# A two-layer hybrid transformer block: x feature-major in the first stage, the modulation matrix in transfers of 2 MB, first projection group of 768 columns

## The chip, the core and the metric

One NeuronCore of a Trainium2 chip runs the whole program. Its engines are TensorE (PE: matrix products into PSUM, the accumulation memory; PEld is its loading of the stationary operand), VectorE (DVE), ScalarE (ACT), GpSimd (POOL) and SyncE (SP), whose queue issues all DMA transfers here. The metric is device time in microseconds (us); lower is better. TensorE's clock is granted at one of two levels, 1.2 or 2.4 GHz; a profile gives the granted clock as a share of the higher one.

## What is computed

```
for l in range(2):                                   # x is 1024 x 2048, f32
    mod = silu(c) @ w_mod[l] + b_mod[l]              # one row, 3 * 2048 columns
    shift, scale, gate = split(mod, 3)
    h = rms_norm(x, g_pre[l]) * (1 + scale) + shift
    proj = h @ w_in[l]                               # 2048 x 5648
    a_q, a_k, a_v, s_u, s_v, c_q, c_k, c_v, c_g, z = split(proj)
    y_a = sliding_window_attention(rope(a_q), rope(a_k), a_v, sinks)
    y_b = gelu(s_u) * mix(layer_norm(gelu(s_v)))     # per 128 tokens
    y_c = rms_norm(gated_linear_attention(c_q, c_k, c_v, log_sigmoid(c_g @ w_up + b)))
    out = (concat(y_a, y_b, y_c) * silu(z)) @ w_out[l]
    x = x + gate * rms_norm(out, g_post[l])
```

`rms_norm(x, g)` is `x / sqrt(mean(x * x) + 1e-6) * g`, the mean taken over the 2048 features of a token.

## The kernel before

The work is cut into four phases (layer 0 and 1, each in two halves of 512 tokens). A phase runs all column groups of `w_in` (mostly 512 columns) and then of `w_out`; attention, gating and linear attention of the phase run beside them as generators that are stepped on by a count of products (`tick`). A projection is done at near f32 accuracy: each operand is split into a high and a low part (ScalarE casts the high part, VectorE subtracts it to get the low one), and for each 128x128 tile of weights and each K tile (128 of the 2048 features, 16 in all) TensorE runs three products, high by high, high by low and low by high (`mm_f`, lines 382 to 384). Instructions are written in program order; a scheduler then sets the order on each engine, and each engine runs its list strictly in that order.

The change touches the first stage alone, which prepares layer 0, tokens 0 to 511. There 8 chunks of `w_mod` (each 16 K tiles by 512 columns, 4 MB: the shift and scale of 256 features) come in 64 transfers of 2 K tiles (tiles `wm`, line 1107's operands; `WM0` = 9 buffers). Each K tile of a chunk is multiplied by `scb` (silu(c), 32 equal columns) into one of four strips of 32 partitions of a PSUM tile; `mod_acc` takes a copy (L1117), four products with the identity matrix turn it (L197), and short VectorE operations make `acol` and `bcol`, the scale and shift per feature (`mod_columns`). x stands token-major in `xg`: ScalarE squares it with a sum per token (L1054), `finish_stats` makes `rstd`, GpSimd multiplies it in (L283), TensorE turns each tile with the identity matrix (L1084), and VectorE and ScalarE make the split operand `act` (L1086, L278, L279). Two K tiles become ready with each chunk.

Between these, generator `work` runs the first projection group, 640 columns in 5 PSUM tiles (`psk`; the products' stationary tiles come from `whl` and, for the fifth, `hl_b`), one step per piece of a chunk. The remaining 128 of the 768 key, query and linear-attention key columns are a group of their own straight after, and then comes the group `vcg` of 272 columns, token-major (lines 390 to 392). `rope_tables(0)` (position angles, sine and cosine: 18 VectorE operations, two sines on ScalarE, two stores on SyncE) is issued at the start of the stage. PSUM has 6 tiles `pj` and 2 tiles `mx`.

Of the kernel before, what the change touches and what calls it, by code (L numbers as in the profile page):

```python
# [10 lines left out]
F32 = mybir.dt.float32  # L11
# [25 lines left out]
WM0 = 9  # L37
# [3 lines left out]
def hybrid_kernel(ctx: ExitStack, tc: tile.TileContext, a, y_out):  # L41
# [82 lines left out]
    def rsqrt(out, src, n):  # L124

        i = sm.tile([P, n], I32, tag="rq_i", name="rq_i")
# [3 lines left out]
        for it in range(3):  # L130
            w = sm.tile([P, n], F32, tag="rq_w", name="rq_w")
            V.tensor_tensor(w, yv, yv, ALU.mult)
            V.scalar_tensor_tensor(w, w, -0.5, src, ALU.mult, ALU.mult)
            dst = out if it == 2 else sm.tile([P, n], F32, tag="rq_y", name="rq_y")
            V.scalar_tensor_tensor(dst, w, 1.5, yv, ALU.add, ALU.mult)
            yv = dst
# [156 lines left out]
    def h_filler_x(h, slots):  # L293
# [456 lines left out]
    def in_phase(l, h, slots, pre=None):  # L750
# [29 lines left out]
        ps = ps[4:] + proj_f(P, slots) if pre else proj_f(256, slots)  # L780
        ck = evac(2, hold, ps)
# [225 lines left out]
    with tc.tile_pool(name="start", bufs=1) as st:  # L1007
        scb = st.tile([P, NK, 32], F32, name="scb")
        V.tensor_copy(scb, sc.unsqueeze(2).broadcast_to([P, NK, 32]))
        xg = [st.tile([P, 4, NT, P], F32, name=f"x0_{g}") for g in range(4)]  # L1010
        ss0 = sm.tile([P, NT, 4], F32, tag="xss4", name="xss4")
        load(mb[0], a["b_mod_col"][0])
        load(gpc[0], a["g_pre"][0])
        ws = deque()
        raw_a, raw_b, hl_a, hl_b = deque(), deque(), deque(), deque()

        def first_load(c):
            if c < 8:
                k = slice(c * KC, (c + 1) * KC)
                pool, tag = (st, "raw_a") if c % 3 == 2 else (wraw_p, "wraw")  # L1020
                r = pool.tile([P, KC, 512], F32, tag=tag, name="raw_a")
                load(r, a["w_in"][0, 0, :, k])
                raw_a.append(r)
                r = st.tile([P, KC, P], F32, name="raw_b", bufs=3)
                load(r, a["w_ck"][0, :, k, 0:P])
                raw_b.append(r)

        def first_split(c):
            if c < 8:
                for raw, hls, cols in ((raw_a, hl_a, 512), (raw_b, hl_b, P)):  # L1030
                    r = raw.popleft()
                    if cols == P:
                        hl = st.tile([P, 2, KC, P], F32R, name="hl_b", bufs=2)
                    else:
                        hl = whl_p.tile([P, 2, KC, 512], F32R, tag="whl", name="whl")
                    S.copy(hl[:, 0], r)
                    V.tensor_tensor(hl[:, 1], r, hl[:, 0].bitcast(F32), ALU.subtract)
                    hls.append(hl)
# [6 lines left out]
        for i in range(WM0 - 1):  # L1045
            mod_load(i)
        for g in range(4):
            load(xg[g], a["x"][0, 4 * g:4 * g + 4].rearrange("j p t c -> p j t c"))
        for _ in rope_tables(0):
            pass  # L1050
        first_load(0)
        for g in range(4):
            for t in range(NT):
                S.activation(junk_tile().rearrange("p (j c) -> p j c", j=4), xg[g][:, :, t], AF.Square,  # L1054
# [217 lines left out]
```

## Time and profile before

| | |
|---|---|
| runs | median 3127.75 us of 3 (3121.66 to 3129.04) |
| profiled execution, its own time | 3122.08 us |
| its span, first to last instruction | 3120.4 us |
| TensorE busy | 3042.7 us of the span |
| mean granted clock | 0.991 |

Rows of the profile are read like this: `L382` is line 382 of the kernel, a line can be a helper's; `out<-in` are the names of tiles; `x8` is a count. A time in square brackets is what the engine idled just before, and what ended that. On TensorE each f32 product of `scb` appears as two records, so a transfer of 2 K tiles is 4 records. Records of products overlap: the start of the next one, not the length, gives the pace.

### The profile page before, as it was taken

To read this page: it belongs to the slowest core of one execution; us is meant where nothing else is said; L and a number is where in the kernel's file an instruction comes from. 1 tells how busy PE (TensorE), PEld (TensorE's weight loads), DVE (VectorE), ACT (ScalarE), POOL (GpSimd) and SP (SyncE) were. 2 spreads that over 40 slices of the span, in tenths; PEclk is the share of its full clock that TensorE was granted. 3 is DMA by queue.
4 is the path that set the end of the run, shared out by engine and by line. 5 is a ranking of instruction groups with operands and counts; after the bars stand their busy time and mean duration, and the time that the engine had idled before them with its cause. 6 is when DMAs were issued, how large, how long until landed. Compare 5 with 4: busy or idle time off the path is not lost.

```text
span 3120.4 us, 44382 instructions
## 1 busy us (share of the span) xinstructions
PE 3042.7 (98%) x17346; PEld 2448.0 (78%) x17346; DVE 1837.3 (59%) x2957; ACT 1206.2 (39%) x2399; POOL 43.4 (1%) x84
## 2 busy tenths in 40 slices
PE   6999999999999999999999999999999999999998
PEld 2477778888878787888888878788888888788886
DVE  3358768565676877745355676644346486663425
ACT  3145437332344443423234554432223544442323
POOL 2000000000000000000000000000000000000000
PEclk8999999999999999999999999999999999999999
DMA  9754446566676435544446323334446332343535
GB/s 330 240 163 140 145 135 206 169 203 203 200 237 197 131 120 178 173 135 149 122 123 190 95 75 94 115 109 142 119 124 203 97 89 85 108 120 113 164 107 165
DMA packets 224195, 468.99 MB, mean 150 GB/s; under 512 B 21584, under 2 KB 77296, under 8 KB 223984
## 3 DMA queue, kind: packets, MB, share of 16 engines
q1 hardware_dynamic: 223984, 466.15, 48.7%
q8 instruction: 136, 2.23, 0.3%
q14 instruction: 75, 0.61, 0.1%
HBM read 429.37 MB, written 36.70 MB: 149 GB/s over the span
## 4 chain that ended last, share of the span: by engine, by line
PE 82%; DVE 8%; DMA 5%; ACT 2%; issue 2%; SPq 0%; DVEq 0%; ACTq 0%
PE pj L382 13%; PE pj L383 12%; PE pj L384 12%; PE pj L390 12%; PE pj L392 12%; PE pj L391 12%; DMA wm<-in_w_mod_dram 2%; PE mx L546 2%; PE mx L492 2%; PE pj L1107 1%; DVE whl L369 1%; DMA t<-in_gla_norm_g_dram 1%; DVE ma L225 1%; DMA t<-in_x_dram 1%; PE mx L533 1%
## 5 line engine op out<-in xcount | busy, mean ns | idle before, releaser
L369 DVE TENSOR_TENSOR whl<-wraw,whl 128x1024 fp32r<-128x1024 f32 (+3 forms) x512 | 590.6, 1154 | 730.6 <-ACT whl L368 728.0
L368 ACT CAST whl<-wraw 128x1024 fp32r<-128x1024 f32 (+3 forms) x512 | 509.1, 995 | 1097.0 <-PE pj L392 515.5
L390 PE MATMUL pj<-whl,act 128*128 128x512 f32 (+1 forms) x2048 | 785.5, 384 | 1.0 <-ACT whl L368 1.0
L392 PE MATMUL pj<-whl,act 128*128 128x512 f32 (+1 forms) x2048 | 777.8, 380 | 0.0
L391 PE MATMUL pj<-whl,act 128*128 128x512 f32 (+1 forms) x2048 | 775.3, 379 | 1.2 <-DVE whl L369 1.2
L382 PE MATMUL pj<-act,whl 128*128 128x512 f32 x1904 | 751.6, 397 | 3.6 <-ACT whl L368 2.0
L383 PE MATMUL pj<-act,whl 128*128 128x512 f32 x1904 | 745.3, 391 | 0.3 <-DVE act L279 0.3
L384 PE MATMUL pj<-act,whl 128*128 128x512 f32 x1904 | 744.5, 391 | 0.5 <-DVE whl L369 0.5
L392 PEld LDWEIGHTS pj<-whl,act 128*128 128x128 f32 x2048 | 385.4, 188 | 73.2 <-issue 1.2
L390 PEld LDWEIGHTS pj<-whl,act 128*128 128x128 f32 x2048 | 385.3, 188 | 72.7 <-issue 5.6
L391 PEld LDWEIGHTS pj<-whl,act 128*128 128x128 f32 x2048 | 385.5, 188 | 68.5 <-DVE whl L369 1.9
L382 PEld LDWEIGHTS pj<-act,whl 128*128 128x128 f32 x1904 | 357.5, 188 | 101.3 <-issue 20.3
L384 PEld LDWEIGHTS pj<-act,whl 128*128 128x128 f32 x1904 | 358.1, 188 | 83.7 <-issue 7.1
L383 PEld LDWEIGHTS pj<-act,whl 128*128 128x128 f32 x1904 | 358.2, 188 | 77.7 <-issue 6.2
L225 DVE SCALAR_TENSOR_TENSOR ma<-wm,sc,ma 128x512 f32<-128x512 f32 x240 | 179.7, 749 | 102.5 <-DMA wm<-in_w_mod_dram 100.1
L517 ACT ACTIVATE M<-M,at_nm 128x128 f32<-128x128 f32 x256 | 99.4, 390 | 46.7 <-DVE at_nm L509 42.2
L535 DVE TENSOR_TENSOR PT<-mx,amask 128x1024 f32<-128x1024 f32 x64 | 78.1, 1220 | 22.6 <-PE mx L533 22.6
L1107 PE MATMUL pj<-wm,scb 128*32 128x512 f32 x256 | 67.0, 665 | 24.2 <-DMA wm<-in_w_mod_dram 24.2
L501 DVE COPY_PREDICATED M<-pmask,mx 128x256 f32<-128x256 uint8 x128 | 51.6, 442 | 57.3 <-ACT M L500 48.5
L546 PE MATMUL mx<-PT,v 128*64 128x128 f32 x960 | 68.4, 288 | 13.9 <-DVE PT L535 13.9
L546 PEld LDWEIGHTS mx<-PT,v 128*64 128x64 f32 x960 | 57.5, 143 | 28.3 <-DVE PT L535 16.3
L500 ACT COPY M<-mx 128x256 f32<-128x256 f32 x96 | 32.1, 375 | 101.0 <-PE mx L492 100.7
(230 smaller groups left out, 2421.9 us busy)
## 6 DMA issues: line engine op xcount, KB each, us to landing
wraw<-in_w_in_dram SPq DMA_DIRECT2D x312, 512.0 KB, 3.6
wraw<-in_w_out_dram SPq DMA_DIRECT2D x136, 512.0 KB, 3.6
wm<-in_w_mod_dram SPq DMA_DIRECT2D x256, 256.0 KB, 3.3
wm<-in_w_mod_dram SPq DMA_DIRECT2D x64, 512.0 KB, 6.2
y<-at SPq DMA_DIRECT2D x64, 256.0 KB, 2.7
q<-y SPq DMA_DIRECT2D x64, 256.0 KB, 3.3
q<-x SPq DMA_DIRECT2D x36, 256.0 KB, 2.8
wraw<-in_w_vcg_dram SPq DMA_DIRECT2D x32, 272.0 KB, 2.8
```

The source lines that it names most:

```text
L225: V.scalar_tensor_tensor(acc, ws[k], sc[:, k:k + 1], acc, ALU.mult, ALU.add)
L368: S.copy(hl[:, 0], raw)
L369: V.tensor_tensor(hl[:, 1], raw, hl[:, 0].bitcast(F32), ALU.subtract)
L382: PE.matmul(ps, lhsT=whi, rhs=slot[:, 0], start=(k == 0), stop=False)
L383: PE.matmul(ps, lhsT=whi, rhs=slot[:, 1], start=False, stop=False)
L384: PE.matmul(ps, lhsT=wlo, rhs=slot[:, 0], start=False, stop=(k == NK - 1))
L390: PE.matmul(ps, lhsT=slot[:, 0, c], rhs=whi, start=(k == 0), stop=False)
L391: PE.matmul(ps, lhsT=slot[:, 0, c], rhs=wlo, start=False, stop=False)
L392: PE.matmul(ps, lhsT=slot[:, 1, c], rhs=whi, start=False, stop=(k == NK - 1))
L517: S.activation(Mf[:, k], Mf[:, k], AF.Exp, bias=nm[:, k:k + 1], scale=0.125, accum_out=den[:, k:k + 1])
L546: PE.matmul(yp[64 * p:64 * p + 64, n * P:(n + 1) * P], lhsT=vv[:, g * 64:g * 64 + 64], rhs=pts[p][:, w, n], start=(w == 0), stop=(w == 1 o ...
L1107: PE.matmul(mps[r:r + 32, :], lhsT=scb[:, k], rhs=w[:, kk], start=(k < 4), stop=(k >= 12))
```

## The change

- x of the first half is loaded feature-major (`xq`, from `x_f`, which now holds both halves) ahead of `w_mod`. Its squares are summed over the features by 8 products with a matrix of ones (`sums`), and 1/sqrt is taken on a tile of 128x512 (`r0`; `rsqrt` now works in place and in a given pool). The split operand is made from `xq` directly: times `acol` times `r0`, plus `bcol` (three operations for a K tile). The squares with sums per token, `rstd` of this half, GpSimd's products and the 64 turns of x are gone.
- A chunk of `w_mod` comes as two transfers of 8 K tiles (2 MB) in 3 buffers, and its products run 8 K tiles in a row.
- Weights of the first group come K tile by K tile (512 columns of `w_in` and 256 of `w_ck`), each queued behind a half chunk; the group has 768 columns in 6 PSUM tiles, and the separate group of 128 columns is gone. The PSUM tile of the modulation moves from `pj` to `mx`.
- The order is written out: half chunk, projection of a K tile, half chunk, columns and operands, projection of a K tile. `rope_tables(0)` moves from the start of the stage to behind chunk 5.

```
         def fetch():
-                load(xt, a["x_f"][len(xs)])
+                load(xt, a["x_f"][1, len(xs)])
...
-        ps = ps[4:] + proj_f(P, slots) if pre else proj_f(256, slots)
-        ck = evac(2, hold, ps)
+        ck = evac(2, hold, ps[4:] if pre else proj_f(256, slots))
...
         if (l, h) == (0, 0):
-            seq = [(a["w_ck"][l, :, :, P:], P)] + seq[2:]
+            seq = seq[2:]
...
+        xq = [act_p.tile([P, 2, H], F32, tag="act", name="xq") for _ in range(8)]
+        for c in range(8):
+            load(xq[c], a["x_f"][0, 2 * c:2 * c + 2].rearrange("j p t -> p j t"))
...
+        def first_load(k):
+            if k < NK:
+                r = wraw_p.tile([P, 1, 768], F32, tag="wraw", name="wraw")
+                load(r[:, 0, 0:512], a["w_in"][0, 0, :, k])
+                load(r[:, 0, 512:], a["w_ck"][0, :, k])
+                raw_q.append(r)
...
-        def mod_load(i):
-            if i < 64:
-                w = st.tile([P, 2, 512], F32, name="wm0", bufs=WM0)
-                load(w, a["w_mod"][0, i // 8, :, 2 * (i % 8):2 * (i % 8) + 2])
+        def mod_load(c, part):
+            if c < 8:
+                w = st.tile([P, 8, 512], F32, name="wm0", bufs=3)
+                load(w, a["w_mod"][0, c, :, 8 * part:8 * part + 8])
                 ws.append(w)
...
+        sums = mxt()
+        for c in range(8):
+            sq = st.tile([P, 2, H], F32, name="sq", bufs=2)
+            S.activation(sq, xq[c], AF.Square)
+            s2 = st.tile([P, H], F32, name="s2", bufs=2)
+            V.tensor_tensor(s2, sq[:, 0], sq[:, 1], ALU.add)
+            PE.matmul(sums, lhsT=ones, rhs=s2, start=(c == 0), stop=(c == 7))
+        r0 = st.tile([P, H], F32, name="r0")
+        V.tensor_scalar(r0, sums, 1.0 / D, EPS, ALU.mult, ALU.add)
+        rsqrt(r0, r0, H, st)
+        psk = [pjt() for _ in range(6)]
...
+        def fill(c, mps):
+            acc = st.tile([P, 512], F32, name="mod_acc", bufs=2)
+            S.copy(acc, mps)
             mod_columns(0, c, acc, 4)
+            for j in range(2):
+                k = 2 * c + j
+                xt, b = t2(), bcol[0][:, k:k + 1]
+                V.scalar_tensor_tensor(xt, xq[c][:, j], acol[0][:, k:k + 1], r0, ALU.mult, ALU.mult)
+                s = act_p.tile([P, 2, 512], F32R, tag="act", name="act")
+                S.activation(s[:, 0], xt, AF.Identity, bias=b)
+                V.scalar_tensor_tensor(s[:, 1], xt, b, s[:, 0].bitcast(F32), ALU.add, ALU.subtract)
+                slots.append(s)
...
         for c in range(8):
+            if c:
+                mod_load(c, 1)
+                first_load(2 * c - 1)
+            mps = mxt()
+            mod_products(mps, 0)
+            if c:
+                project(2 * c - 2)
+                mod_load(c + 1, 0)
+                first_load(2 * c)
+            mod_products(mps, 1)
+            with urgent():
+                fill(c, mps)
+            if c:
+                project(2 * c - 1)
+            if c == 5:
+                for _ in rope_tables(0):
+                    pass
```

TensorE, around the end of a chunk's products (`wm0` by `scb`, into the modulation's PSUM tile) and the turn of `mod_acc`, before (numbers behind names are those of buffers):

```order
L1107 MATMUL pj_286<-wm0_723,scb_167 32x512 x2
L383 MATMUL pj_284<-act_824,whl_692 128x512
L384 MATMUL pj_284<-act_824,whl_692 128x512
L382 MATMUL pj_285<-act_824,hl_b_695 128x512
L1107 MATMUL pj_286<-wm0_730,scb_167 32x512 x2
L383 MATMUL pj_285<-act_824,hl_b_695 128x512
L384 MATMUL pj_285<-act_824,hl_b_695 128x512
L1107 MATMUL pj_286<-wm0_737,scb_167 32x512 x2
L1107 MATMUL pj_286<-wm0_744,scb_167 32x512 x2
L197 MATMUL mx_877<-ident_81,mod_acc_858 128x128 x4
L1084 MATMUL mx_896<-ident_81,x0_2_171 128x128 x4
L1107 MATMUL pj_286<-wm0_759,scb_167 32x512 x2
```

And with the change, around the second half of a later chunk (`L1067` are the products with `scb`, 8 K tiles in one row; `L381` to `L383` the three products of a projection):

```order
L1067 MATMUL mx_489<-wm0_484,scb_185 32x512 x8
L381 MATMUL pj_254<-act_460,whl_555 128x512
L382 MATMUL pj_254<-act_460,whl_555 128x512
L381 MATMUL pj_255<-act_460,whl_555 128x512
L196 MATMUL mx_534<-ident_81,mod_acc_532 128x128 x4
L383 MATMUL pj_254<-act_460,whl_555 128x512
L382 MATMUL pj_255<-act_460,whl_555 128x512
L383 MATMUL pj_255<-act_460,whl_555 128x512
L381 MATMUL pj_256<-act_460,whl_555 128x512
L382 MATMUL pj_256<-act_460,whl_555 128x512
L383 MATMUL pj_256<-act_460,whl_555 128x512
```

The products with `scb` stood in runs of 2 K tiles between single projections; they now stand in a run of 8, and the turns of x (`L1084`) are gone.

SyncE's queue over one chunk of the stage, before:

```order
L58 DMA raw_a_591<-in_w_in_dram 128x1024
L58 DMA raw_b_593<-in_w_ck_dram 128x2x128
L58 DMA wm0_598<-in_w_mod_dram 128x1024
L58 DMA wm0_616<-in_w_mod_dram 128x1024
L58 DMA wm0_623<-in_w_mod_dram 128x1024
L58 DMA wm0_630<-in_w_mod_dram 128x1024
L58 DMA wm0_637<-in_w_mod_dram 128x1024
L58 DMA wm0_652<-in_w_mod_dram 128x1024
L58 DMA wm0_659<-in_w_mod_dram 128x1024
L58 DMA wm0_677<-in_w_mod_dram 128x1024
L58 DMA raw_a_698<-in_w_in_dram 128x1024
L58 DMA raw_b_700<-in_w_ck_dram 128x2x128
```

And with the change, from K tile 10's weights on (`wm0` are the half chunks, `t2_760` is the load of the positions, `cs0_0` and `cs0_1` the stores of the two tables):

```order
L57 DMA wraw_705<-in_w_in_dram 128x512
L57 DMA wraw_705<-in_w_ck_dram 128x256
L57 DMA t2_760<-in_positions_dram 128x512
L57 DMA wm0_788<-in_w_mod_dram 128x4096
L57 DMA wraw_790<-in_w_in_dram 128x512
L57 DMA wraw_790<-in_w_ck_dram 128x256
L57 DMA wm0_823<-in_w_mod_dram 128x4096
L57 DMA cs0_0_99<-t2_768 128x512
L57 DMA cs0_1_100<-t2_780 128x512
L57 DMA wraw_825<-in_w_in_dram 128x512
L57 DMA wraw_825<-in_w_ck_dram 128x256
```

Eight transfers of a chunk became two, one K tile's weights (two transfers) stand behind each, and the positions' load and the tables' stores now stand between the last half chunks, the stores ahead of K tile 12's weights and of the last half chunk.

VectorE where the tables are made, before (between chunk 0's columns and the first split of weights, `L1037`):

```order
L205 SCALAR_TENSOR_TENSOR acol_103<-mod_t,gpc_109 128x2
L158 CAST t_196<-t_196 128x512
L159 TENSOR_SCALAR t_196<-t_196,fcol 128x512
L163 TENSOR_SCALAR t_200<-t_196 128x512
L164 TENSOR_SCALAR t_200<-t_200 128x512
L165 TENSOR_SCALAR t_200<-t_200 128x512
L270 TENSOR_REDUCE xtot<-xss_173 128x4
L168 SCALAR_TENSOR_TENSOR t_204<-t_200,t_196 128x512
L163 TENSOR_SCALAR t_212<-t_196 128x512
```

And with the change (`L1027` is a split of a K tile's weights, here of K tile 11; `L198` the reduction of the following chunk):

```order
L172 TENSOR_SCALAR t_768<-t_768 128x512
L167 SCALAR_TENSOR_TENSOR t_780<-t_776,t_760 128x512
L173 TENSOR_SCALAR t_768<-t_768 128x512
L168 SCALAR_TENSOR_TENSOR t_780<-t_776,t_780 128x512
L169 SCALAR_TENSOR_TENSOR t_780<-t_776,t_780 128x512
L173 TENSOR_SCALAR t_780<-t_780 128x512
L1027 TENSOR_TENSOR whl<-wraw,whl 128x768
L175 TENSOR_SCALAR t_780<-t_780,fcol 128x512
L198 TENSOR_REDUCE mod_m<-mx 128x4
L201 TENSOR_TENSOR bcol_105<-mod_m,mb_107 128x2
L203 TENSOR_TENSOR mod_t<-mod_m,mb_107 128x2
L204 SCALAR_TENSOR_TENSOR acol_103<-mod_t,gpc_109 128x2
```

The tables' operations stood ahead of all splits; they now stand ahead of K tile 11's split and of chunk 6's columns.

## Rows read from the trace of the kernel before

**Rows 1.** Part 1 of the page: busy time, share of the span, instructions.

```profile
PE 3042.7 (98%) x17346; PEld 2448.0 (78%) x17346; DVE 1837.3 (59%) x2957; ACT 1206.2 (39%) x2399; POOL 43.4 (1%) x84
```

**Rows 2.** Waits of TensorE over the whole span: total, times, longest (us).

```profile
PE pj L1107 <- DMA wm<-in_w_mod_dram: 24.2, 6, 12.5
```

**Rows 3.** TensorE's timeline up to 63 us: start, length, what, idle before.

```profile
6.57 6.09 PE L1107 MATMUL pj<-wm,scb 128*32 128x512 f32 x20 [6.57 <-DMA wm<-in_w_mod_dram]
...
39.39 3.19 PE L1107 MATMUL pj<-wm,scb 128*32 128x512 f32 x6 [4.50 <-DMA wm<-in_w_mod_dram]
...
45.92 1.20 PE L382 MATMUL pj<-act,whl 128*128 128x512 f32 x4
...
62.08 0.97 PE L382 MATMUL pj<-act,whl 128*128 128x512 f32 x3 [1.47 <-ACT act L278]
```

**Rows 4.** Windows of 2 us: window, length, TensorE busy, clock, DMA share, GB/s.

```profile
8.00:10.00 2.00, 2.00 (x10) 1.00 1.03 420
...
26.00:28.00 2.00, 0.00 (x0) 0.50 1.07 390
...
44.00:46.00 2.00, 2.00 (x10) 0.68 0.98 364
46.00:48.00 2.00, 2.00 (x9) 1.00 1.01 408
```

**Rows 5.** TensorE's timeline inside one modulation chunk, columns as in rows 3.

```profile
101.03 0.39 PE L383 MATMUL pj<-act,whl 128*128 128x512 f32 x1
101.26 0.39 PE L384 MATMUL pj<-act,whl 128*128 128x512 f32 x1
101.58 1.05 PE L1107 MATMUL pj<-wm,scb 128*32 128x512 f32 x4
102.56 0.50 PE L382 MATMUL pj<-act,whl 128*128 128x512 f32 x1
102.90 0.39 PE L383 MATMUL pj<-act,whl 128*128 128x512 f32 x1
...
107.92 1.06 PE L1107 MATMUL pj<-wm,scb 128*32 128x512 f32 x8
109.72 0.66 PE L197 MATMUL mx<-ident,mod_acc 128*128 128x128 f32 x4 [0.73 <-ACT mod_acc L1117]
```

**Rows 6.** TensorE's timeline at the end of the first stage, columns alike.

```profile
162.66 0.66 PE L197 MATMUL mx<-ident,mod_acc 128*128 128x128 f32 x4 [0.74 <-ACT mod_acc L1117]
...
165.61 1.20 PE L382 MATMUL pj<-act,whl 128*128 128x512 f32 x4
...
182.16 0.40 PE L384 MATMUL pj<-act,whl 128*128 128x512 f32 x1
183.56 0.65 PE L390 MATMUL pj<-whl,act 128*128 128x272 f32 x3 [1.00 <-ACT whl L368]
```

**Rows 7.** Groups of instructions up to 200 us: busy, mean ns, idle before.

```profile
L1107 PE MATMUL pj<-wm,scb 128*32 128x512 f32 x256 | 67.0, 665 | 24.2 <-DMA wm<-in_w_mod_dram 24.2
...
L1084 PE MATMUL mx<-ident,x 128*128 128x128 f32 x64 | 10.7, 298 | 0.0
...
L1054 ACT ACTIVATE junk<-x 128x512 bf16<-128x512 f32 x16 | 10.1, 629 | 1.5 <-DMA x<-in_x_dram 1.0
...
L197 PE MATMUL mx<-ident,mod_acc 128*128 128x128 f32 x32 | 5.2, 284 | 4.6 <-ACT mod_acc L1117 4.6
...
L169 DVE SCALAR_TENSOR_TENSOR t<-t,t 128x512 f32<-128x512 f32 x2 | 1.4, 684 | 0.0
...
L163 DVE TENSOR_SCALAR t<-t 128x512 f32<-128x512 f32 x2 | 0.8, 423 | 0.0
...
L158 DVE CAST t<-t 128x512 f32<-128x512 int32 x1 | 0.4, 426 | 8.3 <-DMA t<-in_positions_dram 8.3
```

**Rows 8.** What SyncE's queue waited for up to 200 us: total, times, longest.

```profile
SPq L58 <- ACT t L178: 10.5, 2, 8.2
```

**Rows 9.** Windows over all engines: PE, PEld, DVE, ACT, POOL, clock, DMA.

```profile
183.00:200.00 17.00, 16.28 (x128) 16.06 (x129) 12.48 (x25) 6.74 (x11) 0.00 (x0) 1.00 0.76 233
```

More of the change, by code (lines that the diff above doesn't have):

```diff
@@ L1007, in hybrid_kernel @@
     with tc.tile_pool(name="start", bufs=1) as st:
+        load(mb[0], a["b_mod_col"][0])
+        load(gpc[0], a["g_pre"][0])
+        xq = [act_p.tile([P, 2, H], F32, tag="act", name="xq") for _ in range(8)]
+        for c in range(8):
+            load(xq[c], a["x_f"][0, 2 * c:2 * c + 2].rearrange("j p t -> p j t"))
         scb = st.tile([P, NK, 32], F32, name="scb")
         V.tensor_copy(scb, sc.unsqueeze(2).broadcast_to([P, NK, 32]))
-        xg = [st.tile([P, 4, NT, P], F32, name=f"x0_{g}") for g in range(4)]
@@ L1028, in first_split @@
[L1028 to L1038, printed above, removed]
@@ L1077, in tail @@
-        def tail(c, acc):
-            mod_columns(0, c, acc, 4)
-            yield
-            for j in (2 * c, 2 * c + 1):
-                pt = mxt()
-                for t in range(NT):
-                    PE.transpose(pt[:, t * P:(t + 1) * P], xg[j // 4][:, j % 4, t], ident)
-                v = t2()
-                V.tensor_scalar(v, pt, acol[0][:, j:j + 1], bcol[0][:, j:j + 1], ALU.mult, ALU.add)
-                slots.append(split(v))
-                yield
-        todo = work()
-        rest = iter(())
@@ L1091, in hybrid_kernel @@
-        at = [0]
-        def go(n=1):
-            for _ in range(n):
-                if at[0] // 5 < min(len(slots), NK):
-                    at[0] += 1
-                    next(todo)
-        first_split(0)
-        for c in range(8):
-            for q in range(8):
-                mod_load(8 * c + q + WM0 - 1)
-                w = ws.popleft()
-                for kk in range(2):
-                    k = 2 * q + kk
-                    r = 32 * (k % 4)
-                    PE.matmul(mps[r:r + 32, :], lhsT=scb[:, k], rhs=w[:, kk], start=(k < 4), stop=(k >= 12))
-                if q in (2, 3):
-                    h_scale(0, 0, xg[c // 2][:, 2 * (c % 2) + q - 2], G)
-                if c == 0 and q in (2, 5):
-                    first_load(1 + q // 4)
-                if q >= 1:
-                    next(rest, None)
-                go()
-            acc = st.tile([P, 512], F32, name="mod_acc", bufs=2)
-            with urgent():
-                S.copy(acc, mps)
-            go(2)
-            rest = tail(c, acc)
-            if c in (0, 7):
-                for _ in rest:
-                    pass
@@ L1123, in hybrid_kernel, with first_split @@
-        for _ in todo:
-            pass
+        ws, raw_q, hl_q = deque(), deque(), deque()
+        def first_load(k):
[4 more added lines that the diff above has]
+                raw_q.append(r)
+        def first_split():
+            r = raw_q.popleft()
+            hl = whl_p.tile([P, 2, 1, 768], F32R, tag="whl", name="whl")
+            S.copy(hl[:, 0], r)
+            V.tensor_tensor(hl[:, 1], r, hl[:, 0].bitcast(F32), ALU.subtract)
+            hl_q.append(hl)
@@ new lines, in hybrid_kernel, with project, mod_products @@
+        r0 = st.tile([P, H], F32, name="r0")
+        V.tensor_scalar(r0, sums, 1.0 / D, EPS, ALU.mult, ALU.add)
+        rsqrt(r0, r0, H, st)
+        psk = [pjt() for _ in range(6)]
+        def project(k):
+            first_split()
+            if k >= NK - 2:
+                w_load()
+            hl = hl_q.popleft()
+            for m in range(6):
+                mm_f(psk[m], hl, 0, m, slots[k], k)
+        def mod_products(mps, part):
+            w = ws.popleft()
+            for kk in range(8):
+                k = 8 * part + kk
+                r = 32 * (k % 4)
+                PE.matmul(mps[r:r + 32, :], lhsT=scb[:, k], rhs=w[:, kk], start=(k < 4), stop=(k >= 12))
@@ L1125, in hybrid_kernel @@
+        first_load(NK - 1)
+        project(NK - 2)
+        project(NK - 1)
+        w_split()
+        w_split()
     load(mb[1], a["b_mod_col"][1])
```

57 lines of the change are left out of this document (8 added, 49 removed).

## The prediction

> **What bounds the kernel now.** The page's busy times come first: TensorE works 3042.7 of 3120.4 us [rows 1], so what remains idle is 77.7 us, and everything else that a change can win must be TensorE's own work. The waits of TensorE tell where the idle time is: 24.2 us of it are products of the modulation that wait for `w_mod`, the longest 12.5 us [rows 2]. TensorE's timeline puts them in the first stage: products start at 6.57 us, one idle of 4.50 us ends at 39.39, and the first projection starts only at 45.92 [rows 3]. From there on TensorE is the bound of the stage: the turn of `mod_acc` comes at 109.72 and at 162.66 [rows 5, 6], three chunks apart, 17.6 us a chunk, with 0.73 us idle at each. The first group of 768 columns is done when the last product ends at 182.16 + 0.40, and the next group starts at 183.56 [rows 6]. The second view to read is the timeline inside a chunk [rows 5]: products of a projection start 0.23 us apart, but a run of four records of the modulation (two K tiles) stands between starts at 101.26 and 102.90, where two plain steps would take 0.46. Such a run costs 1.64 - 0.46 = 1.18 us. A run of eight records (four K tiles, one in each strip) lasts 1.06 us where one of four lasts 1.05 [rows 5]: four strips go at once, and the runs of two K tiles use only half of that. DMA is not the bound after 46 us, but while it has work it moves 390 to 420 GB/s [rows 4].
>
> **The new stage, built from these rows.** I count to the first product of the group of 272 columns, 183.56 us before.
>
> *Start.* The first `w_mod` load of 0.52 MB is in use at 6.57 us [rows 3]. Now x (4.19 MB) and the first two half chunks (2.10 MB each) must have landed before chunk 0 is complete: 8.39 MB, at 400 GB/s 6.57 + 7.87/0.4 = 26.2 us; the third half chunk lands 5.2 us later, at 31.5. TensorE has little to do until then. In before, after the last products of chunk 0, the clock stands at 0.50 in 26:28, and after the wait that ended at 39.39 it is 0.68 in 44:46 and 1.00 in 46:48 [rows 3, 4]; I take the lower level up to about 38 us. A half chunk is two runs of four K tiles, 1.18 + 1.0 = 2.2 us at the full clock, 4.2 at the lower. So chunk 0 is multiplied at 30.4. From there to the first projection with the new operand the last chunk of before shows 0.74 + (165.61 - 162.66) = 3.7 us [rows 6]; with slower turns 4.4, so the operand stands at 34.8. TensorE by then runs the third half chunk (from about 32.4, 4.2 us), so projections start at 36.6, 9.3 us earlier than before.
>
> *Projections.* 16 K tiles by 18 products at 0.227 is 4.1 us each. The first loses about 1.5 us to the lower clock: 36.6 + 4.1 + 1.5 = 42.2. Then come 13 half chunks at 2.2 (28.6), 15 K tiles at 4.1 (61.2), 7 turns of `mod_acc` at 0.6 (4.2; one lasts 0.66 [rows 6]). The copy of `mod_acc`, 0.73 us of idle in before, lies beside three products of the next projection. Sum 136.2.
>
> *The tables.* Their 18 VectorE operations (6 of the kind of 684 ns, 12 near 423 [rows 7], 9.3 us) stand ahead of K tile 11's split, and the sines ahead of ScalarE's half of it. From chunk 5's last products to K tile 11 TensorE has 13.4 us of other work (two half chunks, two K tiles); splits and operands of two K tiles (some 6.5 us of VectorE) come first, so the split is about 2 us late, and I take 2. Both ends: 0 if VectorE gets ahead, and at most 17 (9.3 plus the 8.3 that VectorE waited for the positions [rows 7]) if none of it is covered. SyncE's queue waited 10.5 us for the two sines [rows 8]; now the last half chunk and three K tiles of weights stand behind them. With three buffers the transfers run some 9 us ahead (below), which covers it.
>
> *The end.* Chunk 7's operands are needed after K tile 13's projection, 4.7 us against 3.7 for the chain; with a split of weights in between I take 0.5 us, and 1.0 for other semaphore gaps. The six tiles of the group must be emptied before the next group writes its four, but the first four are complete 1.4 to 3.4 us before the last product (0.69 us a tile): 0.5 us. In all 136.2 + 2 + 0.5 + 1 + 0.5 = 140.2, against 183.56: 43.4 us less.
>
> *Check by differences.* Projections start 9.3 us earlier. About 46 runs of two K tiles at 1.18 (54) become 13 half chunks (28.6): 26 us. 56 of the 64 turns of x fall away; their records sum to 10.7 us and overlap [rows 7], so I take 8. The idle 0.73 at five chunks, 1.47 at 62.08 and 1.00 at 183.56 fall, 6; the tables and ends cost 4 and the lower clock 1.5. 9.3 + 26 + 8 + 6 - 5.5 = 44.
>
> *Costed at nothing.* The sum over features (8 squares of 1024 elements, at most 1.26 us each by the 629 ns for half of it [rows 7], hidden by x's landing; 8 products of ones, at most 1.1 us each; then 1/sqrt in 11 VectorE operations, 7 us by the kinds of rows 7) ends near 28 us, and is first used at about 33; without that cover it costs its excess. GpSimd's products go away off the path. Transfers: up to the last half chunk 43.6 MB must land, at 400 GB/s at 114.4, while TensorE asks for it at about 123; SyncE may issue a half chunk as soon as the one three before it is multiplied, some two halves (13 us) ahead of need.
>
> The Trainium skill ("DMA: Bandwidth & Descriptors", section "Rules for kernel authors") asks for 1 MiB or more per transfer, and its fit of 2.0 us plus bytes over 436 GB/s ("Anatomy of one DMA") would make 64 transfers of 0.52 MB 205 us and 16 of 2 MB 109, an estimate. The trace does not agree: 0.52 MB transfers queued behind each other move 420 GB/s in 8:10 [rows 4], so the larger ones win nothing in my sum.
>
> *Afterwards.* The rotation and splitting of the keys ran beside the group of 128 columns; it now runs beside the group of 272. VectorE was busy 12.48 of 17 us there [rows 9] and gets some 8 more in 24. I take 0.5 us given back, bounds 0 and 8.
>
> The profiled execution took 3122.1 us, 1.7 more than its span; less 43 it is 3079. The median of the runs lies 5.7 above it (3127.75), its fastest run 0.4 below; I forecast a median between, **3082 us**.
>
> **The rivals.**
> 1. *The tables stall the stage* [rows 7, 8]: if the sines hold SyncE's queue long enough that the last half chunk is late, and VectorE's wait for the positions is not covered, 15 us more: 3097. For it: both waits are in the rows. Against: the run-ahead.
> 2. *Given back in the second group*: 8 us more, 3090 [rows 9].
> 3. *Four strips do not go at once over 8 K tiles*: each pair of K tiles then costs 1.0 and a half chunk 4.1; 13 times 1.9 is 25 us, 3107. Against: the run of eight records [rows 5].
> 4. *DMA sets the pace*: at 330 GB/s the last half chunk lands at 137, plus 15 us of work behind it, 152: 3094. It decides below some 370 GB/s; of the busy windows, one (44:46) moved 364, the others more [rows 4].
> 5. *Slower: the waits for 2 MB transfers keep TensorE at the lower clock.* If it idles long enough before each half chunk, 94 us of products (28.6 + 61.2 + 4.2) take 188, and the stage ends near 232: 3171. It passes the old time when 43 us of these 94 run at the lower level. For it: the idle that ended at 39.39 was followed by 0.50 [rows 3, 4]. Against: the idle of 1.47 us at 62.08 came between full-speed products, their steps 0.23, and where TensorE is the bound no wait is longer. And bursts of 6.5 us against transfers of 6.2 (2.49 MB at 400 GB/s) leave hardly a wait. The Trainium skill ("TensorE: Matmul & The Clock Gate", section "HAM oscillation") describes just this case, short bursts between waits for DMA that fall back each time. In the first 46 us the trace agrees with it (0.50 after long waits [rows 4]), after that not.
> 6. *No effect*: if the 128 columns and the start moved nothing, 3125; the removed work stands on TensorE's path, so hardly.
>
> **How the numbers follow.** Forecast 0.70 (its own range 3071 to 3090: a half chunk with its K tile and half a turn is 2.2 + 4.1 + 0.3 = 6.6 us, 0.3 either way is 4 over 13, and the median of runs lies 0 to 6 us above), rival 1 0.10, rival 2 0.08, rival 3 0.05, rival 4 0.03, rival 5 0.03, rival 6 0.01. The range 3068 to 3098 leaves out rivals 3, 5 and 6 and a little of each side. A measurement tells some 0.3% (9 us) from no change: faster is all but rivals 5 and 6, with a little of rival 3 at same: 0.95; same 0.02; slower 0.03.
>
> **What would show it.** First projection near 37 us, runs of 16 records in 2.1 us, a chunk each 13 to 14 us, first product of the group of 272 columns near 140, clock 1.00 from 40 us on, the last half chunk landed before it is asked for. Wrong: TensorE waiting on `wm0` after 50 us, VectorE's split of K tile 11 far behind, or idle time in the second group that before did not have.

## The result, and the profile after

The changed kernel takes **3087.09 us** (median; 3085.24 to 3088.58) where the kernel before takes 3126.2: ratio 0.9873, 95% interval 0.9861 to 0.9885. The same kernel measured again (below) gave 3083.06 and 0.9865 (0.985 to 0.9881). The profiled execution took 3088.58 us, its span is 3086.9.

Part 1 of the page, which answers to [rows 1]: TensorE's busy time fell by 31.7 us, its idle time only from 77.7 to 75.9.

```profile
PE 3011.0 (98%) x17298; PEld 2445.5 (79%) x17298; DVE 1844.1 (60%) x2956; ACT 1202.0 (39%) x2367; POOL 24.0 (1%) x68
```

The waits of TensorE over the whole span, as [rows 2] (total, times, longest):

```profile
PE mx L545 <- DVE PT L534: 16.2, 7, 3.7
...
PE mx L491 <- DVE hold L616: 6.7, 4, 4.4
PE mx L1067 <- DMA wm<-in_w_mod_dram: 6.2, 3, 3.0
PE pj L381 <- ACT whl L1026: 3.9, 2, 2.2
```

The 24.2 us of waits for `w_mod` have become 6.2. TensorE's timeline, as [rows 3, 5, 6] (start, length, what, idle before); the last two lines lie in later groups:

```profile
20.70 1.92 PE L1067 MATMUL mx<-wm,scb 128*32 128x512 f32 x16 [1.89 <-DMA wm<-in_w_mod_dram]
25.61 3.59 PE L1067 MATMUL mx<-wm,scb 128*32 128x512 f32 x16 [2.98 <-DMA wm<-in_w_mod_dram]
...
34.24 0.50 PE L381 MATMUL pj<-act,whl 128*128 128x512 f32 x1 [1.69 <-ACT whl L1026]
...
38.55 1.92 PE L1067 MATMUL mx<-wm,scb 128*32 128x512 f32 x16
...
51.39 1.92 PE L1067 MATMUL mx<-wm,scb 128*32 128x512 f32 x16
53.25 0.50 PE L381 MATMUL pj<-act,whl 128*128 128x512 f32 x1
...
54.06 0.62 PE L196 MATMUL mx<-ident,mod_acc 128*128 128x128 f32 x4
...
102.78 1.92 PE L1067 MATMUL mx<-wm,scb 128*32 128x512 f32 x16
106.86 0.50 PE L381 MATMUL pj<-act,whl 128*128 128x512 f32 x1 [2.16 <-ACT whl L1026]
...
120.84 1.92 PE L1067 MATMUL mx<-wm,scb 128*32 128x512 f32 x16 [1.33 <-DMA wm<-in_w_mod_dram]
...
135.83 0.28 PE L389 MATMUL pj<-whl,act 128*128 128x272 f32 x1
...
994.32 0.35 PE L491 MATMUL mx<-kh,qs 128*128 128x256 f32 x1 [4.40 <-DVE hold L616]
...
1238.29 3.04 PE L545 MATMUL mx<-PT,v 128*64 128x128 f32 x26 [2.84 <-DVE PT L534]
```

A run of 16 records (eight K tiles) lasts 1.92 us, the turn of `mod_acc` at 54.06 stands behind three products of the next K tile without idle, and the group of 272 columns starts at 135.83 with no wait: 47.7 us earlier than the 183.56 of [rows 6]. Yet the span is only 33.5 us shorter. To see where the rest went, count the projection products from the end of both programs and compare the times of the same product. The lead (how much earlier the changed kernel starts a product) is 47.7 us at the start of the 272 columns, 48 at 822 us, 44.2 at 909, 39.3 at 1011, 40.0 at 1138, 33.0 at 1260, and from there on it stays. So some 15 us are given back in these two executions between 820 and 1290 us, in the layer's second half of tokens.

Of the 47.7 us, 11.7 are the earlier first projection (34.24 against 45.92). The last step of 1/sqrt for x is a landmark there. VectorE before, with the change, and in the kernel before with x feature-major alone (an experiment below):

```profile
40.82 0.16 DVE L135 SCALAR_TENSOR_TENSOR rstd<-rq_w,rq_y 128x4 f32<-128x4 f32 x1
```

```profile
26.31 0.69 DVE L134 SCALAR_TENSOR_TENSOR r<-rq_w,rq_i 128x512 f32<-128x512 f32 x1
```

```profile
44.90 0.69 DVE L135 SCALAR_TENSOR_TENSOR r<-rq_w,rq_i 128x512 f32<-128x512 f32 x1
```

In the first and the third, x is queued behind eight transfers of `w_mod`, and the tables' operations and the splits of weights stand between the steps of 1/sqrt; here x comes first and the steps follow each other. Which of the two brings how much was not tried.

Windows of the changed kernel (window, length, TensorE busy, clock, DMA share, GB/s), to be read with [rows 4]:

```profile
24.00:28.00 4.00, 2.39 (x12) 0.70 0.98 418
28.00:32.00 4.00, 3.20 (x28) 0.87 1.02 414
32.00:36.00 4.00, 2.31 (x16) 1.00 0.96 405
60.00:90.00 30.00, 30.00 (x166) 1.00 1.02 417
...
107.50:110.90 3.40, 3.40 (x12) 0.50 0.36 115
...
994.30:998.00 3.70, 3.68 (x15) 0.59 0.48 180
```

Of the modulation's 16 runs only the one at 25.61 (3.59 us) lies at the lower clock. Behind the wait of 4.40 us at 994 the granted clock is 0.59 for 3.7 us, so a wait can cost more than its idle time. The wait of 2.16 us at 106.86 did, too: the clock stood at 0.50 from 107.5 to 110.9, and from 106.86 to the next run (113.27) it took 6.41 us, where the same work took 4.79 at 53.25.

SyncE's queue at the tables, which answers to [rows 8] (start, length, what):

```profile
106.12 3.10 SPq L57 DMA_DIRECT2D cs<-t  x2
...
110.31 0.35 SPq L57 DMA_DIRECT2D wm<-in_w_mod_dram  x1
```

The last half chunk is issued only behind the two stores of the tables, lands 10.5 us later, and TensorE waits 1.33 us for it at 120.84. ScalarE in the same place:

```profile
104.17 1.28 ACT L177 ACT_TABLE_LOAD   x1 [7.34 <-DVE t L173]
105.46 0.63 ACT L177 ACTIVATE t<-t 128x512 f32<-128x512 f32 x1
106.00 0.81 ACT L1026 CAST whl<-wraw 128x768 fp32r<-128x768 f32 x1
```

K tile 11's split (L1026) stands behind the first sine, which needs VectorE's steps of the tables and the loading of its function table (1.28 us); ScalarE stood idle for 7.34 us before them, and TensorE waits 2.16 us for the split.

VectorE shortly before the wait at 994:

```profile
978.71 1.54 DVE L224 SCALAR_TENSOR_TENSOR ma<-wm,sc,ma 128x512 f32<-128x512 f32 x2 [2.16 <-DMA wm<-in_w_mod_dram]
...
990.38 0.75 DVE L224 SCALAR_TENSOR_TENSOR ma<-wm,sc,ma 128x512 f32<-128x512 f32 x1
...
992.18 0.74 DVE L224 SCALAR_TENSOR_TENSOR ma<-wm,sc,ma 128x512 f32<-128x512 f32 x1
992.96 2.48 DVE L616 COPY_PREDICATED hold<-gmask,mx 32x128 f32<-32x128 uint8 x8
```

Line 224 is the lane of later modulation chunks: VectorE adds up `w_mod` K tile by K tile. It waits 2.16 us for such a weight, and two more of its steps stand ahead of the masked copies of line 616, for which TensorE waits. The theory tested first says what puts them there: the lane starts after a fixed 60 ticks, and the group of 128 columns, which used to pass 16 of them first, is gone. So the lane stands 16 ticks later against every group, and its VectorE work falls in other places.

### The profile page after: what moved, and what is told of

Read it like the earlier page. It is cut to its first block, busy times and chain, and to the rows that moved or that the text cites. A ratio compares the mean times of both kernels' runs of the same rounds, so it can differ in the third digit from the quotient of the medians.

```text
span 3086.9 us, 44111 instructions
## 1 busy us (share of the span) xinstructions
PE 3011.0 (98%) x17298; PEld 2445.5 (79%) x17298; DVE 1844.1 (60%) x2956; ACT 1202.0 (39%) x2367; POOL 24.0 (1%) x68
## 4 chain that ended last, share of the span: by engine, by line
PE 78%; DVE 9%; DMA 7%; ACT 3%; issue 2%; SPq 0%; DVEq 0%; ACTq 0%
PE pj L381 13%; PE pj L382 12%; PE pj L383 12%; PE pj L389 11%; PE pj L391 11%; PE pj L390 11%; DMA wm<-in_w_mod_dram 4%; PE mx L545 2%; DVE whl L368 2%; PE mx L491 1%; DVE ma L224 1%; DMA t<-in_gla_norm_g_dram 1%; ACT M L516 1%; PE mx L1067 1%; ACT whl L367 1%
## 5 line engine op out<-in xcount | busy, mean ns | idle before, releaser
L368 DVE TENSOR_TENSOR whl<-wraw,whl 128x1024 fp32r<-128x1024 f32 (+2 forms) x504 | 587.0, 1165 | 696.8 <-ACT whl L367 690.7
L367 ACT CAST whl<-wraw 128x1024 fp32r<-128x1024 f32 (+2 forms) x504 | 505.9, 1004 | 1095.0 <-PE pj L391 525.8
L381 PE MATMUL pj<-act,whl 128*128 128x512 f32 x1920 | 762.9, 397 | 7.4 <-ACT whl L1026 3.9
L383 PE MATMUL pj<-act,whl 128*128 128x512 f32 x1920 | 750.3, 392 | 2.4 <-DVE whl L368 2.0
L382 PE MATMUL pj<-act,whl 128*128 128x512 f32 x1920 | 751.5, 391 | 1.0 <-issue 1.0
L381 PEld LDWEIGHTS pj<-act,whl 128*128 128x128 f32 x1920 | 361.7, 188 | 106.3 <-issue 23.7
L383 PEld LDWEIGHTS pj<-act,whl 128*128 128x128 f32 x1920 | 361.7, 188 | 81.2 <-DVE whl L368 4.2
L382 PEld LDWEIGHTS pj<-act,whl 128*128 128x128 f32 x1920 | 362.1, 189 | 74.5 <-issue 3.0
L491 PE MATMUL mx<-kh,qs 128*128 128x256 f32 (+1 forms) x256 | 67.1, 292 | 9.3 <-DVE hold L616 6.7
## 6 DMA issues: line engine op xcount, KB each, us to landing
wm<-in_w_mod_dram SPq DMA_DIRECT2D x16, 2048.0 KB, 13.7
```

What stands on the lines that cost most here:

```text
L367: S.copy(hl[:, 0], raw)
L368: V.tensor_tensor(hl[:, 1], raw, hl[:, 0].bitcast(F32), ALU.subtract)
L381: PE.matmul(ps, lhsT=whi, rhs=slot[:, 0], start=(k == 0), stop=False)
L382: PE.matmul(ps, lhsT=whi, rhs=slot[:, 1], start=False, stop=False)
L383: PE.matmul(ps, lhsT=wlo, rhs=slot[:, 0], start=False, stop=(k == NK - 1))
L491: PE.matmul(sps[p][:, b, k0:], lhsT=qs[:, p, n * P:(n + 1) * P], rhs=keys[2 * j + p][:, n * P + k0:n * P + 256], start=(part == 0), stop=( ...
```

## The experiments

**The lane's start.** In the changed kernel, and the other way about in the kernel before, where 60 becomes 76:

```diff
-    start("mod", iter((60,)))
+    start("mod", iter((44,)))
```

> The changed kernel with the lane of modulation chunks 8 to 11 and of the second layer started after 44 ticks instead of 60. The group of 128 columns, whose 16 ticks used to pass first, is gone; with 44 the program on TensorE is, from the third group on, instruction for instruction that of the kernel before (12,563 of 12,877 rows). Theory A: some 15 us of the stage's gain are given back between 880 and 1290 us of the changed kernel because the lane stands 16 ticks later against every later group. Then the lead over the kernel before stays at 47 to 49 us to the end, and the run takes 3070 to 3077 us. Rival B: the time is given back because the stage ends earlier and transfers meet other work, whatever the order: 3084 to 3090 us, and the lead falls from 48 to 33 us as it did.

> The kernel before with only the lane's start moved, from 60 ticks to 76: its later order on TensorE is that of the changed kernel (12,564 rows), and the first stage is as it was. Theory A (the order gives the time back): slower than before by 12 to 17 us, 3138 to 3143 us. Rival B (the earlier end of the stage does it): the time of before, 3122 to 3129 us.

Measured: 3088.02 us, ratio 0.9876 (0.9862 to 0.989), for the changed kernel with 44; 3131.94 us, ratio 1.0013 (1.0004 to 1.0022), for the kernel before with 76. The second shows a cost of the order alone, 4.1 us (1.3 to 6.9), a quarter to a third of what theory A expected. (Its trace lies 12.7 us behind the first trace of the kernel before: two single executions overstate it.) TensorE and VectorE of the kernel before with 76, at the place of the changed kernel's wait at 994 (line numbers are one higher here):

```profile
1039.48 0.35 PE L492 MATMUL mx<-kh,qs 128*128 128x256 f32 x1 [4.83 <-DVE hold L617]
...
1283.08 3.67 PE L546 MATMUL mx<-PT,v 128*64 128x128 f32 x30 [2.66 <-DVE PT L535]
```

```profile
1037.35 0.74 DVE L225 SCALAR_TENSOR_TENSOR ma<-wm,sc,ma 128x512 f32<-128x512 f32 x1
1038.12 2.47 DVE L617 COPY_PREDICATED hold<-gmask,mx 32x128 f32<-32x128 uint8 x8
```

The same two waits, in a kernel whose first stage is that of before: they belong to the order. In the first run they went (1.35 us at the first place, none at the second), and the lead lost only 2.5 us between 829 and 1255 us. But it had already lost 7.3 us by 470 us, in the first half of the tokens, 4.4 of them between 212 and 349 us, where one wait stands out. TensorE and VectorE there:

```profile
227.81 0.45 PE L491 MATMUL mx<-kh,qs 128*128 128x128 f32 x1 [5.03 <-DVE hold L616]
```

```profile
224.25 0.49 DVE L222 TENSOR_SCALAR ma<-wm,sc 128x512 f32<-128x512 f32 x1 [2.26 <-DMA gate<-ma]
...
225.79 0.74 DVE L224 SCALAR_TENSOR_TENSOR ma<-wm,sc,ma 128x512 f32<-128x512 f32 x1
226.45 2.46 DVE L616 COPY_PREDICATED hold<-gmask,mx 32x128 f32<-32x128 uint8 x8
```

The lane, started earlier, waits here for its own store (`ma` has one buffer), and the same copies are late. So theory A holds for the place and the mechanism of these waits, and fails as a remedy: moving the lane moves the waits. The time of the first run, 3088.02, lies in rival B's range, and the lead at the stage, 48.3 us, had shrunk to 39 or 40 in the time although the order was that of before. So the lane's 16 ticks are not shown to be all that the changed kernel gives back, and B is not excluded for the rest.

**Each kernel once more.**

> The changed kernel once more, unchanged, to see which of its waits between 815 and 1265 us belong to the kernel and which to one execution. Theory: two of them belong to the later order of VectorE's work that the lane's shift by 16 ticks brings, and stand here again with the same size: 4.4 us near 994 us and 2.5 to 2.8 us near 1238 us; the others there (3.58 near 827, 2.11 near 974) vary. The time is 3084 to 3089 us. Rival: all of the idle time there is one execution's, and the two waits are absent or of other size.

> The kernel before once more, unchanged. Theory: no wait of 4 us stands near 1039 us nor one of 2.5 us near 1283 us, where the kernel before with its lane shifted showed 4.83 and 2.66; idle time between 860 and 1300 us is 13 to 20 us, so that an execution alone moves some 5 us of it; 3122 to 3133 us. Rival: the two waits appear here too, and the order has no part in them.

Measured: 3083.06 us, ratio 0.9865 (0.985 to 0.9881), for the changed kernel; 3125.45 us for the kernel before. The changed kernel's timeline has both waits again, at their places, 0.3 and 0.8 us longer than in the first profile, and its time lies just under the expected range:

```profile
992.53 0.39 PE L491 MATMUL mx<-kh,qs 128*128 128x256 f32 x1 [4.74 <-DVE hold L616]
...
1237.45 2.83 PE L545 MATMUL mx<-PT,v 128*64 128x128 f32 x24 [3.64 <-DVE PT L534]
```

VectorE of the kernel before, once more, at the place of the first:

```profile
1033.62 1.23 DVE L369 TENSOR_TENSOR whl<-wraw,whl 128x1024 fp32r<-128x1024 f32 x1
1034.88 2.49 DVE L617 COPY_PREDICATED hold<-gmask,mx 32x128 f32<-32x128 uint8 x8
```

No step of the lane stands ahead of the copies, and no wait of TensorE follows. Idle time between 860 and 1300 us is 16.7 us here against 13.7 in the first profile, so one execution moves some 3 us of it. The other waits of the stretch vary, too: 3.58 at 827 us in the first profile of the changed kernel, none over 1 us there in the second. Even so, a wait at that place (1.6 to 3.6 us) stands in seven of the nine profiles with the later lane, and in none of the five with the lane of before.

**Runs of four K tiles in the kernel before.** The core of the edit (the loop over the transfers is halved to match, with two steps of the projection for each):

```diff
-WM0 = 9
+WM0 = 5
-                w = st.tile([P, 2, 512], F32, name="wm0", bufs=WM0)
-                load(w, a["w_mod"][0, i // 8, :, 2 * (i % 8):2 * (i % 8) + 2])
+                w = st.tile([P, 4, 512], F32, name="wm0", bufs=WM0)
+                load(w, a["w_mod"][0, i // 4, :, 4 * (i % 4):4 * (i % 4) + 4])
```

> The kernel before with the first stage's modulation weights loaded four K tiles at a time (32 transfers of 1.05 MB, five buffers) instead of two, so that every run of products holds four K tiles, one in each strip. The 128 columns, the time-major x and its 64 turns stay, and so does the later order on TensorE. Theory: a run of four K tiles costs the 1.18 us of a run of two, so some 23 to 24 runs fall away, 24 to 28 us; the group of 272 columns starts at 156 to 160 us instead of 183.6 and the run takes 3098 to 3104 us. Rival: a run's cost goes with its K tiles, and what was saved in the changed kernel came from elsewhere: 3124 to 3129 us.

Measured: 3108.36 us, ratio 0.994 (0.9927 to 0.9954); the 272 columns start at 165.99, 17.6 us earlier (1.3 of it at the start). TensorE over one chunk (two of its four runs are shown):

```profile
102.09 0.66 PE L197 MATMUL mx<-ident,mod_acc 128*128 128x128 f32 x4 [0.76 <-ACT mod_acc L1119]
...
103.67 1.06 PE L1107 MATMUL pj<-wm,scb 128*32 128x512 f32 x8
107.33 1.06 PE L1107 MATMUL pj<-wm,scb 128*32 128x512 f32 x8
...
116.38 0.66 PE L197 MATMUL mx<-ident,mod_acc 128*128 128x128 f32 x4 [0.76 <-ACT mod_acc L1119]
```

Twice the products in 1.06 us, so the theory's mechanism holds; its count was too high. A chunk had seven runs before, one of them of four K tiles already [rows 5], and has four now: three fall away, 14.3 us a chunk against the 17.6 of before, 1.1 us for each. The time keeps what the stage won (17.8 us between the medians, 14.4 to 22.8 by the ratio), so here, with the lane of before, an earlier end of the stage cost nothing afterwards that the noise would let one see.

**x feature-major alone, in the kernel before.** The core of the edit (loads and sums of squares as in the changed kernel):

```diff
-                for t in range(NT):
-                    PE.transpose(pt[:, t * P:(t + 1) * P], xg[j // 4][:, j % 4, t], ident)
-                V.tensor_scalar(v, pt, acol[0][:, j:j + 1], bcol[0][:, j:j + 1], ALU.mult, ALU.add)
-                slots.append(split(v))
+                V.scalar_tensor_tensor(xt, xq[c][:, j - 2 * c], acol[0][:, j:j + 1], r0, ALU.mult, ALU.mult)
+                S.activation(s[:, 0], xt, AF.Identity, bias=bc)
+                V.scalar_tensor_tensor(s[:, 1], xt, bc, s[:, 0].bitcast(F32), ALU.add, ALU.subtract)
```

> The kernel before with x alone changed: feature-major, its sums of squares by products of ones, no turns of x; the 128 columns and the modulation's 64 transfers with their runs of two K tiles stay. Theory: 56 turns of x off TensorE's path are 8 us, and the start changes little, since the loads stand in the same order: 3116 to 3121 us. Rival: x's turns were hidden, or their place is taken by waits for the operand's longer chain: 3124 to 3130 us.

Measured: 3129.26 us, ratio 1.0007 (0.9998 to 1.0015): no gain. Projections start at 48.39, 2.5 us later; from there to the 272 columns it is 131.95 us against 137.64, 5.7 less, and TensorE now waits for the operand's chain in a chunk:

```profile
110.54 1.20 PE L382 MATMUL pj<-act,whl 128*128 128x512 f32 x4 [1.27 <-ACT act L1089]
```

Six such waits, 5.2 us, take back part of the turns. The 272 columns start 3.2 us earlier, and the later groups do not keep that. In the changed kernel a K tile's projection and a half chunk stand between, and there is no such wait.

**Small transfers**, in every chunk (there n is 2 throughout) and in chunk 0 alone:

```diff
-                load(w, a["w_mod"][0, c, :, 8 * part:8 * part + 8])
+                n = 2 if c == 0 else 8
+                for i in range(0, 8, n):
+                    load(w[:, i:i + n], a["w_mod"][0, c, :, 8 * part + i:8 * part + i + n])
```

> The changed kernel with each half chunk of the modulation loaded by four transfers of 0.52 MB instead of one of 2.10 MB; buffers and products as they are, the queue has 48 issues more. Theory A (the size of a transfer wins nothing, since transfers queued behind each other move 390 to 450 GB/s at either size): the time of the changed kernel within 3 us, 3084 to 3091 us, and the first products start earlier. Rival (each transfer has a fixed cost that the large ones save): the stage is paced by DMA; at 330 GB/s the last half chunk lands some 20 us later, 3100 us or more.

> The changed kernel with chunk 0 alone loaded by eight transfers of 0.52 MB instead of two of 2.10 MB; from the second chunk on the order on TensorE is that of the changed kernel (12,843 of 12,881 rows). Theory: the products of chunk 0 begin when the first quarter has landed, the turn of chunk 0 comes 1 to 2 us earlier and so do the projections, 32.5 to 33.5 us instead of 34.24; 3085 to 3087 us, and the group of 272 columns starts near 135. It also says whether the loss with small transfers everywhere lay in the transfers or in the order of the turns: if the transfers themselves were slow, the start would be late here, after 35 us.

Measured: 3092.21 us, ratio 0.9891 (0.9878 to 0.9905), with small transfers everywhere; 3083.18 us, ratio 0.9863 (0.985 to 0.9877), in chunk 0 alone. The first misses both expectations. Its projections start earlier (33.50) and its 272 columns later (143.66, by 7.8 us). Its windows and TensorE's timeline:

```profile
32.00:60.00 28.00, 25.16 (x132) 1.00 1.03 404
60.00:90.00 30.00, 28.44 (x162) 1.00 1.01 384
```

```profile
51.88 1.92 PE L1068 MATMUL mx<-wm,scb 128*32 128x512 f32 x16
54.56 0.66 PE L196 MATMUL mx<-ident,mod_acc 128*128 128x128 f32 x4 [0.76 <-ACT mod_acc L1072]
```

After 32 us no product waits for a transfer. What is lost is the turn's place: the scheduler, which orders by its own estimate, puts it straight behind the chunk's products, where it waits 0.7 us for the copy of `mod_acc`. A chunk takes 14.0 to 14.5 us against 12.84. So this run does not isolate the transfers' size, but it prices the place of the turn, 8.6 us from the first projection to the 272 columns. With small transfers in chunk 0 alone the order is kept, and nothing that can be measured changes: first projection at 34.70, 272 columns at 136.64, no gain at the start either.

**The tables in pieces**, alone and with the small first chunk:

```diff
+        tab = rope_tables(0)
...
             if c:
+                next(tab, None)
                 project(2 * c - 1)
-            if c == 5:
-                for _ in rope_tables(0):
-                    pass
+                next(tab, None)
```

> The changed kernel with the rotation tables made in nine pieces over chunks 1 to 5 instead of in one piece behind chunk 5; the later order on TensorE stays. If the tables are what cost 2.16 us at K tile 11 and 1.33 us at the last half chunk, both waits go and the group of 272 columns starts 3 to 4 us earlier, at 132 to 133 us; the time falls by as much, to 3083 to 3085 us. Rival: VectorE is full in every chunk and the pieces only delay the splits of other K tiles, so that the waits come back in smaller parts: the group starts at 135 to 137 us, 3086 to 3089 us.

> The changed kernel with the tables in pieces and chunk 0 in small transfers, one buffer for the lane's sums as before; the later order on TensorE is that of the changed kernel (12,653 of 12,882 rows). Theory: the 12 us lost with two buffers came from the lane running ahead and moving VectorE's later order, not from the two edits of the first stage; then the group of 272 columns starts at 132 to 134 us and the run takes 3079 to 3084 us. Rival: the first stage's edits cost later what they win, 3086 us or more.

Measured: 3084.67 us, ratio 0.9868 (0.9853 to 0.9883), alone; 3083.52, ratio 0.9865 (0.9848 to 0.9881), with both. The waits of 2.16 and 1.33 us are gone, and the 272 columns start at 133.61 and 134.67. From the seventh chunk's second half on (102.78 above) it is 27.8 us against 33.1 (3.5 of it the two waits, some 1.6 the lower clock behind the first), but the pieces cost 2.5 us in the chunks before, where VectorE's splits are late. At the stage 2.2 us are won, less than theory, and in the whole nothing that these measurements separate from the changed kernel.

**Two edits meant to free VectorE.** Two buffers for the lane's sums, and the copies of line 616 put first, each on top of both edits above:

```diff
-("ma", 1)
+("ma", 2)
```

```diff
-            for e, c in parts:
-                V.copy_predicated(
+            with urgent():
+                for e, c in parts:
+                    V.copy_predicated(
...
```

> The changed kernel with the tables in pieces, chunk 0 in small transfers, and two buffers instead of one for the sums of the lane of modulation chunks, so that VectorE no longer waits for a chunk's store before it starts the next. The first two are worth 3 to 4 us at the end of the first stage (132 us). Theory: of the time given back between 820 and 1290 us, part is VectorE work held up behind the waits for those stores; with two buffers 3 to 6 us of it stay: 3076 to 3081 us. Rival: the stores cost nothing and the waits of that stretch only move: 3082 to 3086 us.

> As the run with both edits of the first stage, and with the masked copies of line 616, which empty the two short accumulators, put ahead of other VectorE work that is ready. Theory: TensorE's waits of 4 to 5 us for them (near 994 us in the changed kernel) go or shrink to under 2 us, and 3 to 8 us of the time with them: 3073 to 3080 us. Rival: another operation becomes late in their place, as with the two buffers, and the time rises: 3085 to 3100 us.

Measured: 3099.4 us, ratio 0.9918 (0.9905 to 0.993), with two buffers, against the theory and 16 us more than with one buffer and the same two edits (3083.52). The stage is as good (132.25), but the lane runs ahead (by 13 to 16 of its steps, counted at the same products) and the waits for VectorE grow, as TensorE's waits show (total, times, longest):

```profile
PE mx L545 <- DVE PT L534: 18.7, 7, 5.5
PE mx L491 <- DVE hold L616: 12.2, 7, 4.7
```

With the copies first: 3082.16 us, ratio 0.9858 (0.9843 to 0.9873), the best median of all but within the others' intervals. It tells nothing of its theory: at the place in question the copies still stand behind the same steps of line 224, and TensorE waits 5.79 us.

## Why the prediction was right

The range and the direction held. The mechanism of the new stage is seen step by step in the trace, and in part shown by runs; two sizes were off, with opposite signs. That the number came so near is partly luck.

The stage, 135.83 against the forecast 140.2, in four parts: the first projection at 34.24 instead of 36.6 (2.4 us better); its K tile 4.3 us instead of 5.6, since the lower clock was over by 32 us (1.3 better); ten steps of a half chunk, a K tile and half a turn from 38.55 to 102.78, 6.42 us each instead of 6.58 (1.6 better); and the rest 33.05 instead of 32.2, with the tables' waits of 2.16 and 1.33 us and some 1.6 at the lower clock (0.9 worse). Together 4.4 us.

Of the 47.7 us, the start is 11.7; between the first projection and the 272 columns, runs of four alone gave 16.3 and x feature-major alone 5.7 in the kernel before. If these add up, the other 14.0 (runs of eight instead of four, the operand's chain and the turn behind other products) were tried by themselves only in the place of the turn.

- *Runs.* Four strips at once are shown by the kernel before with runs of four K tiles: 1.1 us a run, where 1.18 was taken; a run of eight K tiles costs 1.9 to 2.0, not 2.2. Rival 3 falls.
- *Turns of x.* Taken as 8 us; alone they left 5.7 in the stage, with 5.2 of waits for the operand's chain already taken off, and nothing in the whole. In the changed kernel, whose order leaves time for that chain, no such wait stands.
- *The copy of `mod_acc` beside products.* Right, and larger than its 0.73 us a chunk: 8.6 us went over seven chunks when the turn lost that place.
- *The tables.* 2 us was right for the split. "The run-ahead covers it" was wrong for SyncE: rival 1's wait came, at 1.33 us (2.30 in the second profile) instead of 15. In pieces the tables cost 2.0 to 2.8 us less.
- *Larger transfers win nothing.* No run speaks against it: with 0.52 MB the queue moved 404 and 384 GB/s and nothing waited for it, and in chunk 0 alone the size changed nothing. The size of the transfer alone, at the same order of work throughout, was not tried. The Trainium skill's fit ("DMA: Bandwidth & Descriptors", section "Anatomy of one DMA"), which the page gives for single DMAs issued from GpSimd, would by the prediction's estimate have made that kernel's loads some 100 us longer; the measurement differs.
- *DMA and the lower clock* (rivals 4 and 5): DMA gave 405 to 418 GB/s, and from 32 us on the clock of the stage stood at 1.00 except from 107.5 to 110.9, behind a wait for ScalarE and not, as in rival 5, for a transfer. In the second profile the same wait (2.17 us) had no such stretch behind it. (Rival 5's 3171 is 3 us short of its own terms: 3082 and 92.)
- *Afterwards*, 0.5 us given back: **the step that failed.** The lead of 47.7 us became 39 in the median of the first measurement and 43.6 in the second, so 4 to 9 us were given back. The prediction looked for it in the next group, where 1.0 us (2.8 in the second profile) went by 200 us; most of it came some 700 us later. There the lane's 16 ticks, which the prediction did not follow at all, put two waits. The order alone costs 4.1 us (1.3 to 6.9) in the kernel before, and its two waits stand in all nine profiles whose lane lies 16 ticks later (4.4 to 6.2 us and 1.9 to 3.6 us) but in none of the five with the lane of before (at most 1.35 us at those places). How much of the 4 to 9 us is the lane's in the changed kernel stays open: with the lane put back it gave back as much in other places. Between executions a kernel's time moves by several us, and both profiles of the changed kernel are slower than the median of their runs, so the 15 us of the first pair of traces overstate it.

So 3082 came out near the measured 3083 and 3087 because a stage 4.4 us better than forecast paid for what the later groups gave back.

## What to carry to other kernels

Where a counter of ticks or steps decides when background work is issued, taking out a group shifts that work against everything behind it: compare the order far downstream, not just at the seam, and align two traces by counting the same instructions from the end to see where a gain goes. Products with 32 of 128 columns can run four abreast only when they stand next to each other (here four K tiles took 1.06 us and two 1.05), so load their weights in units that make them ready together. A small step such as the turn of an accumulator hides its wait only behind work that does not depend on it (1.2 us a chunk here, 0.7 of it the wait), and an edit elsewhere can move it out of that place.

## What the runs showed of the hardware

Eight K tiles in four strips take 1.92 us, four take 1.06 and two 1.05, each at clock 1.00: with one product in a strip, four strips last as long as two, and the second product in each strip adds 0.86 us. One wait of 4.40 us in a stretch where TensorE was otherwise busy was followed by 3.7 us at a granted clock of 0.59; the section "HAM oscillation" of the Trainium skill's page "TensorE: Matmul & The Clock Gate" describes the same for waits on DMA, and here VectorE caused it. A shorter wait, 2.16 us for ScalarE at 106.86, was followed by 3.4 us at 0.50 in one profile of the changed kernel, and its like of 2.17 us by none in the other.
